# Moving two thirds of the modulation vector's matrix-vector products from the preceding feed-forward stage into the layer that uses them

## The chip, the cores and the metric

One core of a Trainium2 chip runs the whole program. The metric is the device time of one execution in microseconds (us); where several executions are given, their median counts. A core has five engines that run their own instruction streams in order and wait for each other by semaphores: TensorE (PE: matmuls; its weight loads are shown as PEld), VectorE (DVE), ScalarE (ACT), GpSimd (POOL) and SyncE (SP), which here issues all loads and stores.

## The reference, cut to what matters

The program is one inference step through two trunk layers for 640 tokens (512 latent, 128 context) of width 1024. In each layer a conditioning vector is turned into six modulation vectors of 1024 each (shift, scale and gate of the mixers, shift, scale and gate of the feed-forward part), for the latent and for the context condition:

```
def adaln(cond, w_ada, b_ada):
    m = jax.nn.silu(cond) @ w_ada + b_ada          # w_ada (1024, 6144), one per layer
    return [t[:, None, :] for t in jnp.split(m, 6, axis=-1)]

sh1, sc1, g1, sh2, sc2, g2 = mod
h = rms_norm(x) * (1 + sc1) + sh1                  # blocks 0-7 (shift) and 8-15 (scale)
... four mixers from h @ w_in: latent attention (MLA), a recurrence (HGRN), neighbourhood
    attention (NA), grouped-query attention (GQA)
x = x + g1 * merge_branches(...)                   # blocks 16-23
h2 = rms_norm(x) * (1 + sc2) + sh2                 # blocks 24-31 and 32-39
x = x + g2 * ((silu(gate_ffn) * a) @ w_ffn_out)    # blocks 40-47
```

A block is 128 entries of the modulation vector, so a layer has 48 blocks, and a block's weights are 512 KB.

## The kernel before, in words

Activations lie with channels on the 128 partitions and the 640 tokens along the free axis, in two halves of 384 and 256 columns. Every matmul of the large projections runs three times on values split in a high and a low part, so TensorE has by far the most work. A layer goes through these stages: a preparation of the latent attention (`mla_pre`), then sixteen mixers `j` = 0 to 15 in the order MLA 0-3 (phase `ph` 0), HGRN 4-7 (phase 1), NA 8-11 (phase 2), GQA 12-15 (phase 3), then the merge, the output projection `out`, the second norm, and the feed-forward stage.

A mixer is a Python generator that yields between its pieces: an attention mixer (`attn_pair`) 18 times, an HGRN mixer (`hgrn_mix`) 11 times. `weave` runs one such generator and, after each yield, as much of a filler (the projections for the next mixer, the gates, the branch projections) as keeps pace. In an attention mixer a unit is: scores on PE into `pss`; row maximum on DVE (`sm`, L218); exponential on ACT (`P`, L235); reciprocal and scaling on DVE (L231, L232); a unit later the transposes on PE (`pst`, L81) and their split into `ph` (ACT) and `pl` (DVE, L176). Each weight block is loaded by SP into `wraw` (two buffers, L117) and split by ACT and DVE into `whi` and `wlo` (L123). In an HGRN mixer seven levels follow each other, each with matmuls into `pss`, a masked copy on DVE (`hA`, L804) and small products on DVE and POOL (L817 to L824); its last DVE instruction is L882.

The modulation blocks are made by `ada_tail` as row products on DVE, not on PE. For each item it loads a piece of a block (`ada`, L982) and multiplies it on DVE with the two conditions and sums it (L984; two of these *products* per item, each followed by a short read of the accumulator, `aacc`). With `parts` = 4 an item is 128x256 (128 KB), with 2 it is 128x512 (256 KB). The conditions themselves are loaded from `crow` at the start of each part (L978). The weights go through a ring of `depth` pieces, so the load of an item waits until DVE is done with the item `depth` before it, and SP's later loads stand behind it.

The Python order is not the order of execution: when the program is built, a scheduler orders the instructions of every engine. It may put an instruction ahead of others that were written earlier, where its inputs are there and the engine would have nothing else. In the kernel before, `along` draws three items of layer 0's blocks 16 to 39 after each yield of mixers 4 to 7; the feed-forward stage of layer 0 makes layer 0's blocks 40 to 47 and all 48 blocks of layer 1, four items after each hidden block (`hidden`) and two after each output block (`back`). Layer 1 makes none in its own stages. That makes the two layers a natural pair for comparison: the same work with and without the products.

Of the kernel before, what the change touches and what calls it, by code (L numbers as in the profile page):

```python
# [7 lines left out]
F32 = mybir.dt.float32  # L8
# [19 lines left out]
NH = FFN // 128  # L28
# [36 lines left out]
class Trunk:  # L65
# [1025 lines left out]

    def along(self, main, side, n):

        try:
            while True:
                yield next(main)
                for _ in range(n):
                    next(side, None)
        except StopIteration as e:
            return e.value  # L1100
# [22 lines left out]
    def mixers(self, l, first):  # L1123
# [27 lines left out]

        self.weave(rest(), early(), 15360 * len(EARLY), 70000)
        outs, nxt = None, []
        for j in range(16):
# [9 lines left out]
            main = mix.pop(j)()  # L1164
            if l == 0 and 4 <= j < 8:
                if j == 4:
                    ada = self.ada_tail(0, 16, 40, 4, 2)
                main = self.along(main, ada, 3)
            nxt.append(self.weave(main, f, wp + wm, steps[ph]))
            if j % 4 == 3:  # L1170
                outs, nxt = self.split_outs(nxt), []
        for d in range(8):
            for _ in self.merge(l, order[3], d, outs, gates):
                pass
        self.drop(outs)

    def layer(self, l, hs, first):
# [49 lines left out]
        nxt = l + 1 < self.depth  # L1227
        def ada():
            if l == 0:
                yield from self.ada_tail(0, 40, 48, 2, 4, True)  # L1230
            if nxt:
                yield from self.ada_tail(l + 1, 0, 48, 2, 4, True)

        ada = ada()

        def back(halves, last=False):
            for m in range(8):
# [6 lines left out]
                for c0, c1 in halves:  # L1244
                    self.resid(x[m], self.gemm(w, [fs[j] for j in range(g0, g1)], c0, c1), l, 40, m, c0, c1)
                    yield 3 * (g1 - g0) * (c1 - c0)
                if g1 < NH:
                    for _ in range(2):
                        next(ada, None)

        ws = []
        for g0, g1 in KGROUPS:
            for j in range(max(g0, 2), g1):
                sum(hidden(j, HALVES, None))
                for _ in range(4):
                    next(ada, None)
            if g1 < NH:
                sum(back(HALVES))
                self.drop([fs[j] for j in range(g0, g1)])
# [39 lines left out]
    def run(self):  # L1299
        nc, tc, A = self.nc, self.tc, self.A  # L1300
        with (
# [24 lines left out]
            self.trash = cst.tile([128, 256], BF16, name="trash")  # L1326
            self.aacc = cst.tile([128, 192], F32, name="aacc")
            self.mod = [cst.tile([128, 48, 2], F32, name=f"mod{l}") for l in range(self.depth)]
# [205 lines left out]
```

## Time and profile before

| what | value |
|---|---|
| time before, median of 3 runs | 3157.28 us (3156.32 to 3160.29) |
| the profiled execution's own time | 3160.58 us |
| its span in the profile | 3158.8 us |
| mean granted TensorE clock | 0.994 of full |
| PE busy | 3042.6 us (96%) |
| DVE busy | 2183.3 us (69%) |
| ACT busy | 1467.5 us (46%) |
| POOL busy | 286.0 us (9%) |

The span is what the views below divide into stretches, counted from its first instruction; 1.8 us of the execution lie outside it. PE's ends are modelled, so a busy PE is not PE at its peak.

### The profile page before, as it was taken

How to read it: one execution, taken by the hardware profiler on the slowest of the kernel's cores; microseconds unless marked ns; L12 is line 12 of the kernel's file. 1: busy time of each engine (PE TensorE's matmuls, PEld its weight loads, DVE VectorE, ACT ScalarE, POOL GpSimd, SP SyncE). 2: the span in 40 equal slices, each digit the busy share in tenths (PEclk: the TensorE clock that was granted, in tenths of full speed). 3: DMA queues.
4: the chain of work that ended last, by engine and by line, in shares of the span. 5: the costliest groups of instructions: out<-in, count | busy, mean ns of one | idle time of the engine just before them, and what ended most of it. 6: DMA issues, size and time to landing. Idle time of an engine off the chain costs nothing.

```text
span 3158.8 us, 54167 instructions
## 1 busy us (share of the span) xinstructions
PE 3042.6 (96%) x20898; PEld 2934.2 (93%) x20898; DVE 2183.3 (69%) x4894; ACT 1467.5 (46%) x3090; POOL 286.0 (9%) x301
## 2 busy tenths in 40 slices
PE   8999989899999999999998999999999999999998
PEld 4899988899899999999998999989988999999998
DVE  5676988877877577676867776678778766533335
ACT  4565433556765352121346654446576644422222
POOL 1100222110111010000001002221011100000000
PEclk9999999999999999999999999999999999999999
DMA  6211333232111345454521112213311124322222
GB/s 216 66 62 63 118 114 113 81 103 89 48 41 59 124 154 161 147 163 146 167 91 60 60 61 74 73 58 97 98 61 44 46 68 160 101 81 70 78 76 72
DMA packets 135121, 297.16 MB, mean 94 GB/s; under 512 B 15888, under 2 KB 53584, under 8 KB 134864
## 3 DMA queue, kind: packets, MB, share of 16 engines
q1 hardware_dynamic: 134864, 293.71, 28.9%
q8 instruction: 165, 2.70, 0.4%
q14 instruction: 92, 0.75, 0.1%
HBM read 276.70 MB, written 16.95 MB: 93 GB/s over the span
## 4 chain that ended last, share of the span: by engine, by line
PE 71%; DVE 15%; ACT 5%; issue 4%; DMA 4%; POOL 1%; SPq 0%; DVEq 0%; ACTq 0%; POOLq 0%
PE psg L78 58%; PE pss L78 7%; PE pst L81 3%; PE pst L78 3%; DVE wlo L123 2%; DVE trash L984 2%; ACT P L235 1%; DVE pl L176 1%; DMA ada<-in_w_ada 1%; ACT whi L84 1%; DVE nx L1054 1%; DMA wada<-in_w_adak 1%; PE pst L167 1%; DVE sm L218 1%; DVE P L232 1%
## 5 line engine op out<-in xcount | busy, mean ns | idle before, releaser
L78 PE MATMUL psg<-hh,whi 128*128 128x384 f32 (+1 forms) x3776 | 1121.1, 315 | 7.5 <-DVE ft L1209 4.5
L78 PE MATMUL psg<-hl,whi 128*128 128x384 f32 (+1 forms) x3776 | 1109.0, 312 | 2.8 <-DVE hl L1056 2.4
L78 PEld LDWEIGHTS psg<-hh,whi 128*128 128x128 f32 x3776 | 717.0, 190 | 10.6 <-DVE ft L1209 5.1
L78 PEld LDWEIGHTS psg<-hl,whi 128*128 128x128 f32 x3776 | 717.3, 190 | 4.7 <-DVE hl L1056 3.1
L78 PE MATMUL psg<-hh,wlo 128*128 128x384 f32 (+1 forms) x3744 | 649.5, 312 | 0.0
L84 ACT ACTIVATE whi<-wraw 128x1024 fp32r<-128x1024 f32 (+3 forms) x402 | 380.7, 947 | 457.4 <-PE psg L78 365.7
L78 PEld LDWEIGHTS psg<-hh,wlo 128*128 128x128 f32 x3744 | 569.5, 190 | 0.0
L123 DVE TENSOR_TENSOR wlo<-wraw,whi 128x1024 fp32r<-128x1024 f32 (+3 forms) x398 | 455.1, 1144 | 123.0 <-ACT whi L84 112.4
L235 ACT ACTIVATE P<-pss,sm 128x768 f32<-128x768 f32 (+2 forms) x240 | 163.0, 680 | 202.2 <-DVE sm L218 114.5
L176 DVE TENSOR_TENSOR pl<-pst,ph 128x384 fp32r<-128x384 f32 (+2 forms) x408 | 196.4, 510 | 24.6 <-ACT ph L84 20.2
L84 ACT ACTIVATE ph<-pst 128x384 fp32r<-128x384 f32 (+2 forms) x408 | 170.4, 457 | 49.4 <-PE pst L81 46.2
L81 PE MATMUL pst<-ident,P 128*128 128x128 f32 x1104 | 168.3, 275 | 16.5 <-DVE of L242 11.3
L1070 DVE SCALAR_TENSOR_TENSOR xr<-psg,mod,xr 128x128 f32<-128x128 f32 (+1 forms) x192 | 78.6, 436 | 152.0 <-PE psg L78 151.9
L218 DVE TENSOR_REDUCE sm<-pss 128x1 f32<-128x768 f32 x128 | 122.0, 953 | 53.6 <-PE pss L78 52.6
L984 DVE CUSTOM_DVE_ANT_0 yada<-ada 128x512 f32<-128x512 f32 x224 | 154.4, 689 | 5.1
L81 PEld LDWEIGHTS pst<-ident,P 128*128 128x128 f32 x1104 | 125.6, 140 | 31.2 <-DVE of L242 17.6
L78 PE MATMUL psg<-oTh,whi 128*128 128x384 f32 (+1 forms) x512 | 153.0, 316 | 0.1
L78 PE MATMUL psg<-oTl,whi 128*128 128x384 f32 (+1 forms) x512 | 152.7, 314 | 0.0
L78 PE MATMUL psg<-fh,whi 128*128 128x256 f32 (+1 forms) x512 | 148.1, 308 | 0.0
L78 PE MATMUL psg<-fl,whi 128*128 128x256 f32 (+1 forms) x512 | 148.1, 308 | 0.0
L84 ACT ACTIVATE fh<-fy 128x384 fp32r<-128x384 f32 (+1 forms) x88 | 41.4, 471 | 179.4 <-DVE fy L1211 179.4
L1211 DVE SCALAR_TENSOR_TENSOR fy<-ft,psg 128x384 f32<-128x384 f32 (+1 forms) x88 | 42.8, 487 | 112.3 <-PE psg L78 111.7
(324 smaller groups left out, 5181.3 us busy)
## 6 DMA issues: line engine op xcount, KB each, us to landing
wraw<-in_w_f SPq DMA_DIRECT2D x128, 512.0 KB, 3.4
wraw<-in_w_in SPq DMA_DIRECT2D x88, 512.0 KB, 3.4
wraw<-in_w_gate SPq DMA_DIRECT2D x64, 512.0 KB, 3.3
ada<-in_w_ada SPq DMA_DIRECT2D x112, 256.0 KB, 3.1
wraw<-in_w_br SPq DMA_DIRECT2D x64, 256.0 KB, 2.6
wraw<-in_w_out SPq DMA_DIRECT2D x32, 512.0 KB, 3.3
ada<-in_w_ada SPq DMA_DIRECT2D x96, 128.0 KB, 2.3
gd<-gt SPq DMA_DIRECT2D x28, 320.0 KB, 2.2
```

What stands on the lines that cost most here:

```text
L78: self.nc.tensor.matmul(out, lhsT, rhs, start=start, stop=stop)
L81: self.nc.tensor.transpose(out, in_, self.ident)
L84: self.nc.scalar.activation(out, in_, AF.Copy, scale=scale)
L123: nc.vector.tensor_sub(lo[:, :n], raw[:, :n], self.r(hi[:, :n]))
L167: self.nc.tensor.transpose(ps[:, i * rows : (i + 1) * rows], t[:rows, c0 + i * 128 : c0 + (i + 1) * 128], self.ident[:rows, :rows])
L176: self.nc.vector.tensor_sub(lo, src, self.r(hi))
L218: nc.vector.tensor_reduce(nm, S[:, 0:n], axis=AX.X, op=ALU.max, negate=True)
L232: nc.vector.tensor_scalar_mul(P[:, p0 : p0 + n], P[:, p0 : p0 + n], l)
L235: self.nc.scalar.activation(P, S, AF.Exp, bias=nm, accum_out=l)
L984: nc.vector.tensor_tensor_reduce(out=y, in0=w, in1=c, scale=1.0, scalar=0.0, op0=ALU.mult, op1=ALU.add, accum_out=acc[:, b, k, j : j + 1])
L1070: self.nc.vector.scalar_tensor_tensor(x[:, a:b], ps[:, a - c0 : b - c0], mod[:, b_g + m, j : j + 1], x[:, a:b], op0=ALU.mult, op1=ALU.add)
L1211: nc.vector.scalar_tensor_tensor(y[:, 0:n], tg[:, 0:n], 0.5, pa, op0=ALU.mult, op1=ALU.mult)
```

## The change

`along` takes a fraction instead of a whole number: it now draws `a` items in `b` yields (3 in 5), with a count that goes on from mixer to mixer. Both layers make blocks 16 to 47 as 128 items of 128x256, drawn along the mixers of phases 0, 2 and 3, that is MLA, NA and GQA; what is left after mixer 15 is made before the merge. The feed-forward stage of layer 0 keeps only blocks 0 to 15 of layer 1 (32 items of 128x512, two after each hidden block and none after `back`). The accumulator tile `aacc` grows from 192 to 256 columns. In all the program has 96 items of 128x256 and 112 of 128x512 before, and 256 and 32 now; the bytes loaded for them are the same (42 MB).

```diff
@@ -1089,12 +1089,13 @@
             sum(fill)
         return res
 
-    def along(self, main, side, n):
+    def along(self, main, side, count, a, b):
 
         try:
             while True:
                 yield next(main)
-                for _ in range(n):
+                count[0] += 1
+                for _ in range(count[0] * a // b - (count[0] - 1) * a // b):
                     next(side, None)
         except StopIteration as e:
             return e.value
@@ -1150,6 +1151,7 @@
             mix[0] = yield from first
 
         self.weave(rest(), early(), 15360 * len(EARLY), 70000)
+        ada, count = self.ada_tail(l, 16, 48, 4, 2), [0]
         outs, nxt = None, []
         for j in range(16):
             ph, q = divmod(j, 4)
@@ -1162,13 +1164,13 @@
             p = prep(j + 1) if j < 15 else None
             f = self.blend(p, wp * (3 if j == 11 else 1), merges(j, outs), wm)
             main = mix.pop(j)()
-            if l == 0 and 4 <= j < 8:
-                if j == 4:
-                    ada = self.ada_tail(0, 16, 40, 4, 2)
-                main = self.along(main, ada, 3)
+            if ph != 1:
+                main = self.along(main, ada, count, 3, 5)
             nxt.append(self.weave(main, f, wp + wm, steps[ph]))
             if j % 4 == 3:
                 outs, nxt = self.split_outs(nxt), []
+        for _ in ada:
+            pass
         for d in range(8):
             for _ in self.merge(l, order[3], d, outs, gates):
                 pass
@@ -1225,13 +1227,7 @@
         self.weave(self.norm_mod(hs, x, l, 24, 32, *HALVES[1]), some(HALVES[0]), 96 * n0, 6)
         sum(some(HALVES[1]))
         nxt = l + 1 < self.depth
-        def ada():
-            if l == 0:
-                yield from self.ada_tail(0, 40, 48, 2, 4, True)
-            if nxt:
-                yield from self.ada_tail(l + 1, 0, 48, 2, 4, True)
-
-        ada = ada()
+        ada = self.ada_tail(l + 1, 0, 16, 2, 4, True) if nxt else iter(())
 
         def back(halves, last=False):
             for m in range(8):
@@ -1244,15 +1240,12 @@
                 for c0, c1 in halves:
                     self.resid(x[m], self.gemm(w, [fs[j] for j in range(g0, g1)], c0, c1), l, 40, m, c0, c1)
                     yield 3 * (g1 - g0) * (c1 - c0)
-                if g1 < NH:
-                    for _ in range(2):
-                        next(ada, None)
 
         ws = []
         for g0, g1 in KGROUPS:
             for j in range(max(g0, 2), g1):
                 sum(hidden(j, HALVES, None))
-                for _ in range(4):
+                for _ in range(2):
                     next(ada, None)
             if g1 < NH:
                 sum(back(HALVES))
@@ -1324,7 +1317,7 @@
                 return t
 
             self.trash = cst.tile([128, 256], BF16, name="trash")
-            self.aacc = cst.tile([128, 192], F32, name="aacc")
+            self.aacc = cst.tile([128, 256], F32, name="aacc")
             self.mod = [cst.tile([128, 48, 2], F32, name=f"mod{l}") for l in range(self.depth)]
             self.crow = dr.tile([2, D], F32, name="crow")
             c = const("cond", "cond")
```

What the scheduler makes of it is seen in the built order. On DVE, in the first MLA mixer of layer 1, around the first two row maxima (`sm<-pss`), before:

```order
L267 RECIPROCAL sm<-sm 128x2
L268 TENSOR_TENSOR P<-P,sm 128x256
L176 TENSOR_TENSOR mv<-psg,mv 128x64
L218 TENSOR_REDUCE sm<-pss 128x1
L176 TENSOR_TENSOR mv<-psg,mv 128x64
L231 RECIPROCAL sm<-sm 128x1
L232 TENSOR_SCALAR P<-P,sm 128x768
L176 TENSOR_TENSOR pl<-pst,ph 128x256
```

and now, at the same place (the `ISA` rows of L984 are the products and the reads of their accumulator):

```order
L218 TENSOR_REDUCE sm<-pss 128x1
L984 ISA trash,aacc<-ada 128x256
L984 ISA aacc 128x1
L176 TENSOR_TENSOR pl<-pst,ph 128x256
L984 ISA trash,aacc<-ada 128x256
L984 ISA aacc 128x1
L231 RECIPROCAL sm<-sm 128x1
L232 TENSOR_SCALAR P<-P,sm 128x768
```

Products moved in between the row maximum and the reciprocal, and to other places of the unit. On DVE, in the first HGRN mixer of layer 1, from its second to its third level, before:

```order
L817 TENSOR_TENSOR hq<-hq,hT 128x40x2x4
L819 TENSOR_TENSOR hq<-hq,hT 128x40x8
L824 TENSOR_TENSOR hT<-hT_22024 128x40 x2
L123 TENSOR_TENSOR wlo<-wraw,whi 128x512
L804 COPY_PREDICATED hA<-hmask,pss 128x640
```

and now:

```order
L824 TENSOR_TENSOR hT<-hT_21922 128x40 x2
L984 ISA trash,aacc<-ada 128x256
L984 ISA aacc 128x1
L984 ISA trash,aacc<-ada 128x256
L984 ISA aacc 128x1
L984 ISA trash,aacc<-ada 128x256
L984 ISA aacc 128x1
L123 TENSOR_TENSOR wlo<-wraw,whi 128x512
L984 ISA trash,aacc<-ada 128x256
L984 ISA aacc 128x1
L804 COPY_PREDICATED hA<-hmask,pss 128x640
```

So products now stand in layer 1's HGRN mixers, although none is drawn along them: the scheduler took them forward. On SP, in layer 1 at the start of the MLA mixers (weight loads of L117, stores of gates of L895), before:

```order
L117 DMA wraw<-in_w_k 128x128
L895 DMA gd_98<-gt 128x640
L117 DMA wraw<-in_w_v 128x256
L117 DMA wraw<-in_w_gate 128x1024
L117 DMA wraw<-in_w_qn 128x256
```

and now:

```order
L117 DMA wraw<-in_w_k 128x128
L978 DMA ada<-crow 128x256 x2
L982 DMA ada<-in_w_ada 128x256
L895 DMA gd_98<-gt 128x640
L117 DMA wraw<-in_w_v 128x256
L982 DMA ada<-in_w_ada 128x256 x2
L117 DMA wraw<-in_w_gate 128x1024
L982 DMA ada<-in_w_ada 128x256 x2
L117 DMA wraw<-in_w_qn 128x256
```

The loads of the items moved in ahead of weight loads of the same stage. Counted over DVE's whole order, with the stretches named by the DVE rows at which they begin (each MLA mixer at its L264, and the HGRN mixers by their ends at L882), the products of 128x256 stand thus:

| stretch of a layer | before, layer 0 | before, layer 1 | now, layer 0 | now, layer 1 |
|---|---|---|---|---|
| preparation, up to the first MLA mixer | 0 | 0 | 11 | 10 |
| MLA mixers 1 to 3 | 0 | 0 | 82 | 83 |
| A: MLA mixer 4 and HGRN mixer 1 | 68 | 0 | 100 | 100 |
| B: HGRN mixer 2 | 62 | 0 | 54 | 54 |
| C: HGRN mixer 3 | 51 | 0 | 9 | 9 |
| D: HGRN mixer 4 | 11 | 0 | 0 | 0 |
| NA and GQA mixers | 0 | 0 | 0 | 0 |

Of the 82 and 83 in MLA mixers 1 to 3, 47 and 45 stand between a row maximum and its reciprocal. The products of 128x512 in the feed-forward stage of layer 0 are 224 before and 64 now.

## Rows read from the trace of the kernel before

**Rows 1.** The page: busy time, share of the span and instructions of each engine.
```profile
PE 3042.6 (96%) x20898; PEld 2934.2 (93%) x20898; DVE 2183.3 (69%) x4894; ACT 1467.5 (46%) x3090; POOL 286.0 (9%) x301
```

**Rows 2.** Busy time by stretch: layer 0's, then layer 1's.
```profile
core 0: us, PE busy (x) PEld busy (x) DVE busy (x) ACT busy (x) POOL busy (x), PEclk, DMA share, GB/s
...
278.90:608.90 330.00, 302.01 (x2103) 289.67 (x2101) 279.08 (x766) 136.00 (x269) 68.52 (x68) 0.98 0.32 102
...
1045.70:1612.40 566.70, 563.57 (x3836) 562.10 (x3835) 411.08 (x888) 178.97 (x267) 12.85 (x12) 1.00 0.47 151
1698.20:1845.90 147.70, 144.62 (x1007) 138.15 (x1008) 114.33 (x244) 93.60 (x224) 0.00 (x0) 0.99 0.19 64
1845.90:2145.90 300.00, 294.92 (x2103) 284.64 (x2102) 197.97 (x378) 136.65 (x269) 67.01 (x68) 1.00 0.21 66
2145.90:2582.40 436.50, 421.35 (x2954) 403.36 (x2953) 333.35 (x808) 266.92 (x650) 46.41 (x51) 1.00 0.21 67
2582.40:3147.90 565.50, 563.32 (x3835) 561.89 (x3833) 259.26 (x437) 173.10 (x260) 8.18 (x8) 1.00 0.28 91
```

**Rows 3.** The same view: stretches A to D of layer 0, then of layer 1.
```profile
278.90:419.20 140.30, 133.29 (x927) 128.97 (x925) 113.14 (x288) 60.37 (x120) 24.41 (x22) 0.99 0.31 97
419.20:495.80 76.60, 69.18 (x484) 67.69 (x485) 65.88 (x199) 26.79 (x48) 16.57 (x17) 0.96 0.38 118
495.80:560.90 65.10, 57.02 (x395) 54.04 (x394) 58.24 (x174) 24.49 (x45) 17.30 (x17) 0.97 0.35 111
560.90:608.90 48.00, 42.52 (x302) 38.97 (x300) 41.82 (x110) 24.35 (x56) 10.23 (x12) 1.00 0.24 75
1845.90:1977.90 132.00, 131.38 (x931) 128.09 (x931) 85.93 (x156) 60.42 (x120) 23.42 (x22) 1.00 0.21 66
1977.90:2044.30 66.40, 66.32 (x478) 64.59 (x477) 39.18 (x75) 27.05 (x48) 16.03 (x17) 1.00 0.22 73
2044.30:2099.20 54.90, 52.91 (x385) 50.99 (x384) 36.50 (x69) 25.20 (x48) 17.23 (x17) 1.00 0.18 57
2099.20:2145.90 46.70, 44.31 (x315) 40.97 (x313) 36.36 (x83) 23.98 (x53) 10.32 (x12) 1.00 0.22 67
```

**Rows 4.** The products of 128x256: duration in ns (min/median/max), first and last start.
```profile
L984 DVE CUSTOM_DVE_ANT_0 trash<-ada x192: 402/424/1772, 324.8 to 572.8; 128x256 bf16<-128x256 f32 x192
```

**Rows 5.** What PE waited for, layer 0 from 278.9 to 608.9 us: total, times, longest.
```profile
PE pss L78 <- DVE hSf L852: 10.5, 3, 5.4
PE pss L78 <- DVE hA L804: 3.8, 6, 0.9
PE pss L81 <- DVE hon L871: 3.6, 3, 1.9
```

**Rows 6.** What DVE waited for, the same stretch.
```profile
DVE trash L984 <- DMA ada<-in_w_ada: 9.0, 13, 1.8
DVE trash L984 <- DMA ada<-crow: 6.7, 5, 1.7
```

**Rows 7.** What SP's loads waited for, the same stretch.
```profile
SPq L982 <- DVE aacc L984: 88.7, 63, 4.8
SPq L117 <- DVE wlo L123: 52.3, 15, 17.1
SPq L117 <- DVE aacc L984: 23.0, 11, 4.0
```

**Rows 8.** What DVE waited for, MLA mixers 1 to 3 of layer 1 (1698.2 to 1845.9 us).
```profile
DVE sm L231 <- ACT P L235: 15.1, 16, 1.1
DVE sm L218 <- PE pss L78: 6.7, 9, 1.1
...
DVE sm L267 <- ACT P L235: 1.7, 2, 0.9
```

**Rows 9.** What PE waited for, the same stretch of layer 1.
```profile
PE pst L81 <- DVE of L242: 2.3, 4, 0.6
```

**Rows 10.** Busy time in the end of layer 1's preparation (columns as in group 2).
```profile
1620.00:1698.20 78.20, 70.64 (x479) 67.07 (x479) 51.98 (x117) 48.12 (x115) 14.94 (x16) 0.98 0.24 79
```

## The prediction

> **What bounds the kernel now.** I read the page first: TensorE is busy 96% of the span, VectorE 69% [rows 1]. So nearly all the time is PE's, and a change that moves only DVE work and loads can act in one way alone: by making PE wait more, or less, for DVE. Where that happens is not seen in the mean, so I cut the span into stages and laid layer 0 beside layer 1, which do the same work [rows 2]. The reader should see two things there. The feed-forward stage is 566.7 us in layer 0 and 565.5 in layer 1, with PE busy 563.6 and 563.3: layer 0 carries 224 products that layer 1 hasn't (DVE 411.1 against 259.3 us), and they cost 1.2 us in all. And the stretch from the fourth MLA mixer to the first NA mixer is 330.0 us in layer 0 and 300.0 in layer 1: here 192 products cost 30.0 us. DVE is busy 279.1 against 198.0 us there, so a product with its accumulator read is 81.1 / 192 = 0.422 us of DVE, which agrees with its own median duration of 424 ns [rows 4].
>
> The waits then say how it becomes time: in that stretch of layer 0 PE waits for DVE's results in the HGRN chain (hSf 10.5, hA 3.8, hon 3.6 us) [rows 5]. DVE itself waits 9.0 + 6.7 = 15.7 us for the products' loads [rows 6]. SP stands 88.7 us in front of product loads, and weight loads behind them wait 23.0 us on products [rows 7]; in front of its other weight loads it waits for buffers.
>
> **A scale for the cost.** The stretch splits into four at the ends of the HGRN mixers, and each layer 0 piece has its layer 1 twin without products [rows 3]. For each I set the products' DVE time against the time that DVE is idle in the twin, and read off what the piece lost:
>
> A: 140.3 - 132.0 = 8.3 us for 68 products, 28.7 us of DVE for 132.0 - 85.9 = 46.1 idle (62% filled): 0.122 us lost for each product.
> B: 76.6 - 66.4 = 10.2 for 62; 26.2 for 27.2 idle (96%): 0.165.
> C: 65.1 - 54.9 = 10.2 for 51; 21.5 for 18.4 idle (117%): 0.200.
> D: 48.0 - 46.7 = 1.3 for 11; 4.6 for 10.3 idle (45%): 0.118.
>
> The loss rises with the filling, and isn't small even at half. These rates hold everything that comes with a product: DVE's delay, the ring's waits, SP's blocked weight loads, and the granted clock, which in B and C of layer 0 is 0.96 and 0.97 of 2.4 GHz, a mean with short spells at 1.2 GHz after PE stood, and 1.00 in their twins. So I don't price those apart.
>
> **The change, part by part.** What decides is where the built order puts the products, by the counts of the table above, not where they are drawn. NA and GQA get none in either layer, so their 436.5 us [rows 2] stay. Each layer now has 82 or 83 in MLA mixers 1 to 3, 100 in A, 54 in B, 9 in C, none in D, and 10 or 11 in the preparation.
>
> *Taken away*: layer 0's stretch loses its present 192 products: -30.0 us. The feed-forward stage loses 160 of 224: 1.2 x 160/224 = -0.9 us. The work that hides the rest is PE itself, which never runs short there. Were that cover gone, all the DVE time of the 64 left would show, 64 x (411.1 - 259.3)/224 = 43 us; PE's 99% says it isn't.
>
> *Added, MLA mixers 1 to 3* (147.7 us, DVE busy 114.3, idle 33.4 [rows 2]). 83 products are 35.0 us, more than the idle time. No row shows products in these mixers, so I bound it. From below: all idle time is used and only the excess shows, 1.6 us. From above: DVE is never busier than in layer 0's stretch, 279.1/330.0 = 84.6%, so the mixers last (114.3 + 35.0)/0.846 = 176.5, +28.8 us. Between them: 46 products stand between a row maximum and its reciprocal, where DVE now idles 15.1 + 1.7 = 16.8 us for the exponential [rows 8]; they need 19.4, so 2.6 us of theirs is left over. The other 37 I charge at the rate of B and C for a filling of 105%, 0.18 us: 6.7. Together 9.3 us. I take this value: the order fits more than half into waits that exist, and PE waits on DVE for little there today (2.3 us on the largest [rows 9]); but 84.6% filled DVE is nearer to what the next mixers show than 100%, so not less.
>
> *Added, A, B, C*: A at 100 x 0.422/46.1 = 92% filled: between the rates of 62 and 96%, 0.160, so 16.0 us. B at 54: 84%, 0.150, 8.1 us. C at 9: 21%, no rate that low, 0.11 at most from D, 1.0 us. Sum 25.1 (at the mean rate 30.0/192 it would be 163 x 0.156 = 25.5).
>
> *Added, preparation*: DVE is idle 78.2 - 52.0 = 26.2 us in its last part [rows 10]; 11 products at 0.11, 1.2 us. Nothing, if they fall in PE's shadow; 4.6 if each shows in full.
>
> *SP's queue*: 160 more loads of 128 KB and 80 fewer of 256 KB. DMA engines are at most 0.47 busy in any of these stretches [rows 2], so the bytes cost nothing. What stands behind a product load now is the next MLA mixer's weights and the gates' stores; its cost is in the rates. That two ring slots stay taken through MLA, the wider `aacc`, and blocks 16 to 47 of layer 1 being made only in layer 1 (their first reader is the output projection, two phases after the last product) I cost at nothing: no row shows a wait on them.
>
> A layer's cost is 9.3 + 25.1 + 1.2 = 35.6 us. Two layers: 71.2; less 30.0 and 0.9: **+40.3 us**. Layer 0 ends about 5 us later than now, layer 1 about 35. The profiled execution's 3160.6 us becomes 3200.9; it stands 3.3 us above the median of the runs, so against the median I forecast 3157.3 + 40 = **3197 us**, its own range 3186 to 3212 as the 9.3 and the 25.1 are each off by up to a third. Chance 0.50.
>
> **The rivals.**
>
> *Neighbours, not filling (0.19).* GpSimd is busy 68.5 us in the stretch where products cost 30.0, and 0.00 us in MLA mixers 1 to 3 [rows 2]; single products take up to 1772 ns against a median of 424 [rows 4]. If the loss comes from products that run beside GpSimd, those in MLA mixers 1 to 3 and the preparation are free and only 163 in a layer pay 0.156: 25.5 us, two layers 51, less 30.9: +20, **3177 us**. Against it: A has the same share of GpSimd (24.4 of 140.3, or 17%) as B (22%) and yet loses a quarter less for each product; the rates follow the filling. The Trainium skill, "SBUF — State Buffer", section "Who interferes with whom", says that a VectorE instruction with two SBUF inputs and a GpSimd instruction that reads SBUF block each other for the whole instruction; a product has two such inputs. The long tail of durations agrees with that rule, and by it this rival's time would be the right one.
>
> *Saturation (0.15).* MLA mixers 1 to 3 reach the upper bound, +28.8, since weight loads come late behind product loads as well: a layer 28.8 + 25.1 + 1.2 = 55.1, +79 in the end, **3236 us**; half of the way from the forecast, 3217. For it: DVE is overfilled by 1.6 us even if no wait of its own is left, and a DVE that runs behind lets SP fall behind.
>
> *The other side: it was the loads (0.08).* Half of the 30.0 us is DVE standing for the ring, 15.7 us [rows 6]. If the new order gives the loads time to land, the rest is 14.3/192 = 0.074 a product; 163 of them cost 12.1 us, those in MLA's waits none: 24.3 - 30.9 = -6.6, **3151 us**, faster. It decides where a layer's whole cost falls below (30.9 - 6.3)/2 = 12.3 us. Against it: SP's order now has product loads ahead of nearly every weight load of these mixers, and the ring is as short as before.
>
> *It does what the words say*: the attention stages take the products and HGRN is free of them. If hidden, that would be -30.9, 3126 us. The built order excludes it: 163 of 256 products stand in stretches A to C.
>
> *No change that can be told (0.08).* Costs between the last two cases and the forecast that happen to meet the gain, 15 us a layer.
>
> **How the numbers follow.** 0.2%, 6.3 us, is about what these runs can tell from no change. Faster by more needs the loads' case: 0.08. Within it: 0.08. The forecast, the neighbours and saturation are all slower: 0.84. For 8 in 10 I leave out the faster case, part of the one without change, and the last third of saturation: 3160 to 3228 us.
>
> **What the profile after would show.** MLA mixers 1 to 3 of both layers near 157 us, with the wait of the reciprocal for the exponential gone from DVE's list; at 148 or 149 the neighbours' or the loads' case is right, at 170 saturation. The stretch A to D near 325 us in both layers, layer 0's slightly below its 330.0, layer 1's up from 300.0, with PE waits on hSf and hA in A and B of layer 1 and none in C and D. NA with GQA unchanged at 436.5 us. The feed-forward stage of layer 0 within 1 us of layer 1's. DVE's wait for `ada` loads of the order of 10 to 25 us a layer. The forecast is wrong if the MLA mixers behave like the feed-forward stage, where 224 products vanish beside a PE that has enough to do, or if the shifted order of PE's own instructions gains or loses by itself.

## The result and the profile after

The changed kernel takes 3177.97 us (median of 4 runs, 3175.21 to 3182.16) where the kernel before took 3158.02 beside it: ratio 1.006, 95% interval 1.0045 to 1.0075. It is slower by about 20 us; 39 to 40 had been forecast. The profiled execution took 3175.21 us with a span of 3173.3, 14.5 more than before's span; it lies 2.8 below its median and before's 2.6 above, which makes up the 20.

The page's line of busy times, which answers to [rows 1]:

```profile
PE 3048.2 (96%) x20898; PEld 2937.9 (93%) x20898; DVE 2191.8 (69%) x5216; ACT 1464.6 (46%) x3086; POOL 294.4 (9%) x301
```

Nothing is to be seen in it: shares stay the same to the percent. The stretches, cut as in [rows 2, 3] (layer 0's MLA mixers 1 to 3, A to D, feed-forward stage, then layer 1's MLA mixers 1 to 3, A, B, C, D, A to D, NA with GQA):

```profile
core 0: us, PE busy (x) PEld busy (x) DVE busy (x) ACT busy (x) POOL busy (x), PEclk, DMA share, GB/s
133.80:285.80 152.00, 145.37 (x1009) 137.16 (x1009) 141.87 (x410) 93.30 (x225) 0.00 (x0) 1.00 0.31 99
...
285.80:604.60 318.80, 297.99 (x2101) 287.23 (x2100) 262.86 (x710) 136.97 (x270) 70.17 (x68) 0.99 0.31 98
...
1041.20:1606.20 565.00, 562.69 (x3830) 561.31 (x3829) 305.86 (x564) 178.22 (x266) 12.79 (x12) 1.00 0.35 112
...
1693.90:1846.00 152.10, 145.08 (x1008) 136.66 (x1008) 142.59 (x412) 93.10 (x225) 0.00 (x0) 1.00 0.31 100
1846.00:1990.50 144.50, 134.57 (x924) 131.00 (x923) 124.80 (x357) 60.74 (x121) 24.57 (x22) 0.96 0.34 110
1990.50:2060.30 69.80, 66.42 (x477) 64.61 (x477) 60.51 (x180) 27.14 (x48) 16.57 (x17) 1.00 0.35 111
2060.30:2113.90 53.60, 52.59 (x380) 50.60 (x381) 41.75 (x92) 24.11 (x44) 18.46 (x17) 1.00 0.23 74
2113.90:2163.10 49.20, 45.27 (x321) 42.30 (x321) 36.89 (x85) 25.11 (x57) 10.27 (x12) 1.00 0.26 74
1846.00:2163.10 317.10, 298.85 (x2101) 288.53 (x2101) 263.94 (x710) 137.10 (x270) 69.86 (x68) 0.98 0.31 98
2163.10:2597.50 434.40, 421.52 (x2960) 403.22 (x2959) 333.55 (x808) 266.28 (x649) 48.98 (x51) 1.00 0.21 67
```

Read down the lengths. MLA mixers 1 to 3 went from 147.7 to 152.0 and 152.1. A to D went from 330.0 to 318.8 in layer 0 and from 300.0 to 317.1 in layer 1. NA with GQA is 2.1 us shorter in layer 1, the feed-forward stage 1.7 and 0.7. DVE in MLA is busy 142.6 of 152.1 us, 94%, and PE still loses only 4.4. A product with its read takes (142.59 - 114.33) / 83 = 0.341 us of DVE there, not 0.422, so the 83 fill 85% of the 33.4 idle and not 105%.

A was the largest term, so I cut it once more, 46 us after its start, where the products of before begin in layer 0 (324.8 us [rows 4]). First the two parts in the kernel before, layer 1, without products:

```profile
1845.90:1891.80 45.90, 45.36 (x309) 44.14 (x309) 29.25 (x53) 22.83 (x48) 4.69 (x3) 1.00 0.15 48
1891.80:1977.90 86.10, 86.02 (x624) 83.95 (x624) 56.68 (x103) 37.59 (x73) 18.73 (x19) 1.00 0.24 76
```

and now:

```profile
1846.00:1892.00 46.00, 44.33 (x302) 43.21 (x302) 40.74 (x118) 22.81 (x50) 6.60 (x5) 1.00 0.28 89
1892.00:1990.50 98.50, 90.24 (x623) 87.80 (x621) 84.06 (x240) 37.93 (x72) 17.97 (x18) 0.95 0.37 119
```

This is a cut by time, so the first part is 46 us long in both. The same instruction of PE, the first on `wlo` behind the scores, starts 45.8 us after the start of A before and 46.6 now: a third of the products cost 0.8 us there, though DVE is 89% busy, and 11.7 of the 12.5 us come later.

Cut at the same work, at the first matmul of HGRN mixer 1 (`pss<-hQ,hkk`) and at GpSimd's second instruction on `hkk` behind the levels, A has three parts. Before, layer 1:

```profile
1845.90:1909.20 63.30, 62.76 (x441) 61.12 (x441) 42.37 (x76) 32.87 (x70) 7.11 (x5) 1.00 0.17 53
1909.20:1952.59 43.39, 43.31 (x310) 42.71 (x309) 28.43 (x54) 16.03 (x31) 12.45 (x14) 1.00 0.25 81
1952.59:1977.90 25.31, 25.31 (x184) 24.26 (x183) 15.12 (x27) 11.52 (x20) 3.86 (x4) 1.00 0.26 75
```

and now:

```profile
1846.00:1916.22 70.22, 65.17 (x440) 63.37 (x439) 60.27 (x175) 33.10 (x71) 7.30 (x5) 0.95 0.31 101
1916.22:1959.58 43.36, 43.28 (x310) 42.72 (x309) 41.23 (x112) 16.02 (x31) 13.22 (x15) 1.00 0.37 119
1959.58:1990.50 30.92, 26.12 (x179) 24.92 (x177) 23.30 (x72) 11.62 (x20) 4.05 (x4) 0.94 0.38 116
```

The middle part, the seven levels, lost nothing, with 29 products in it, DVE busy 95% of the time and GpSimd 30%. The 12.5 us are the 6.9 up to the first level and the 5.6 behind the last one; layer 0 has 7.8, 0.2 and 5.2.

The 6.9 hang on one row maximum of MLA mixer 4. Before, DVE took it as soon as its scores were there, the first row; now it first makes two products among other work, waits 1.60 us for the conditions' row and makes two more products:

```profile
1891.94 0.96 DVE L218 TENSOR_REDUCE sm<-pss 128x1 f32<-128x768 f32 x1 [0.64 <-PE pss L78]
...
1896.73 0.43 DVE L984 CUSTOM_DVE_ANT_0 trash<-ada 128x256 bf16<-128x256 f32 x1 [1.60 <-DMA ada<-crow]
...
1897.55 0.95 DVE L218 TENSOR_REDUCE sm<-pss 128x1 f32<-128x768 f32 x1
```

ACT waits 4.4 us for it and makes `hvf`, a tile of HGRN mixer 1, behind it; PE waits 3.4 us for `hvf`. No instruction of GpSimd runs between 1892.7 and 1919.8 us, and none of the 49 products up to the first level took more than 0.43 us. Layer 0 has the same stand (3.5 us) behind the same wait (1.59).

What a product beside GpSimd looks like, and what then stands behind it, is in the timeline. GpSimd where the third part begins (start, length, engine, line, operation):

```profile
1959.58 1.76 POOL L765 TENSOR_TENSOR hkk<-hk 128x640 f32<-128x640 f32 x1
```

and DVE in 9 us around it:

```profile
1958.65 1.24 DVE L984 CUSTOM_DVE_ANT_0 trash<-ada 128x256 bf16<-128x256 f32 x1
...
1959.94 1.69 DVE L984 CUSTOM_DVE_ANT_0 trash<-ada 128x256 bf16<-128x256 f32 x1
...
1964.43 0.42 DVE L984 CUSTOM_DVE_ANT_0 trash<-ada 128x256 bf16<-128x256 f32 x1 [1.86 <-DMA ada<-in_w_ada]
...
1966.39 1.22 DVE L123 TENSOR_TENSOR wlo<-wraw,whi 128x1024 fp32r<-128x1024 f32 x1
1967.53 0.34 DVE L852 SCALAR_TENSOR_TENSOR hSf<-hSf,hT,pss 128x128 f32<-128x128 f32 x1
```

The product of 1.69 us instead of 0.42 ends 0.3 us after GpSimd's instruction; the two long ones together take 2.1 us more than two others. Behind them DVE works off six more products, waits 1.86 us for a load among them, and comes late to `hSf`, the state of the recurrence, for which PE waits 2.7 us. PE's waits in A to D of layer 1, which answer to [rows 5]:

```profile
PE pss L78 <- DVE hSf L852: 5.1, 2, 2.7
PE pst L167 <- ACT hvf L84: 3.4, 1, 3.4
PE pss L78 <- DVE hA L804: 3.1, 4, 1.4
```

A stand costs more than itself. In the 11 us after the wait of 3.4 us (the first row), and in 13 us around the one for `hSf` above (the second), the granted clock is

```profile
1901.00:1912.00 11.00, 10.85 (x57) 10.57 (x58) 8.10 (x26) 4.38 (x11) 0.00 (x0) 0.72 0.48 165
1967.00:1980.00 13.00, 12.08 (x76) 11.58 (x77) 9.25 (x32) 2.39 (x8) 0.02 (x1) 0.87 0.41 126
```

that is, part of each at 1.2 GHz instead of 2.4. From the matmul that waited for `hvf` to the next ones on `ph` and `mv`, the same work, PE takes 6.65 us where it took 3.94. Over all of A the granted clock of 0.96 would be 5.8 us of work at full speed (0.04 of 144.5); PE's busy time rose by 3.2, from 131.4 to 134.6.

### The profile page after: what moved, and what is told of

It reads as the page before. It is cut to its first block, busy times and chain, and to the rows that moved or that the text cites. A ratio compares the mean times of both kernels' runs of the same rounds, so it can differ in the third digit from the quotient of the medians.

```text
span 3173.3 us, 54661 instructions
## 1 busy us (share of the span) xinstructions
PE 3048.2 (96%) x20898; PEld 2937.9 (93%) x20898; DVE 2191.8 (69%) x5216; ACT 1464.6 (46%) x3086; POOL 294.4 (9%) x301
## 4 chain that ended last, share of the span: by engine, by line
PE 68%; DVE 18%; ACT 5%; DMA 4%; issue 3%; POOL 0%; SPq 0%; DVEq 0%; ACTq 0%; POOLq 0%
PE psg L78 57%; PE pss L78 6%; DMA ada<-in_w_ada 2%; PE pst L78 2%; PE pst L81 2%; DVE wlo L123 2%; DVE trash L984 2%; DVE pl L176 2%; ACT P L235 2%; DVE P L232 1%; DVE sm L218 1%; ACT whi L84 1%; DVE nx L1054 1%; PE pst L167 1%; ACT ph L84 1%
## 5 line engine op out<-in xcount | busy, mean ns | idle before, releaser
L984 DVE CUSTOM_DVE_ANT_0 trash<-ada 128x256 bf16<-128x256 f32 x512 | 234.0, 457 | 51.6 <-DMA ada<-in_w_ada 38.3
L176 DVE TENSOR_TENSOR pl<-pst,ph 128x384 fp32r<-128x384 f32 (+2 forms) x408 | 197.0, 510 | 17.6 <-ACT ph L84 14.5
```

Source lines behind the costliest of these rows:

```text
L176: self.nc.vector.tensor_sub(lo, src, self.r(hi))
L984: nc.vector.tensor_tensor_reduce(out=y, in0=w, in1=c, scale=1.0, scalar=0.0, op0=ALU.mult, op1=ALU.add, accum_out=acc[:, b, k, j : j + 1])
```

## The experiments

Throughout, my theory is that of the forecast: a product costs what DVE's filling makes it cost. The rivals were the loads, GpSimd, and later the place where a product stands. Times are medians beside runs of the kernel before; the ratio is to these. The median of the kernel before was 3158.0 to 3160.6 us beside the different runs, so two times that weren't taken side by side can differ by 2 to 3 us without a cause in the kernel.

**What is there to lose: no products, loads alone, products alone, a deeper ring.** Four kernels, each the change with one edit. Blocks 16 to 47 without loads and products (their values are left out):

```diff
-                for j, c in enumerate((c0, c1)):
+                for j, c in enumerate((c0, c1) if last else ()):
```

with `if last:` ahead of the load as well.

> All loads and products of the items along the mixers are left out (blocks 16 to 47 of the modulation are then only the bias): the floor. By the twins in the kernel before, a layer without products has 300.0 us in A to D and 147.7 in MLA mixers 1 to 3: 3158 - 30 = 3128, and the change's products cost the rest, 50 us, or 25 a layer. All theories agree; it sets the scale for the next three.

Measured 3125.8 us, ratio 0.9887 (0.9873 to 0.9902). This is the floor for everything below. The loads alone (the values again left out):

> The loads of the items stay, with their ring, but no product reads them (blocks 16 to 47 are then only the bias). Filling and neighbours: the loads cost nothing by themselves, the floor within 5 us, 3128 to 3133. Loads (SP's queue held up): 10 us or more above the floor; but without products the ring is freed by the loads themselves, so this shows only what the DMA traffic costs, not the waits for DVE.

Measured 3133.9 us, 0.9912 (0.9898 to 0.9927): 8 us over the floor, between the two expectations. Products alone, with the condition's row in place of the loaded piece (so other values):

> The products stay, but read the rows of the conditions that lie in SBUF, and no pieces of weights are loaded (the modulation is then wrong in blocks 16 to 47). Since nothing waits for a ring, the order takes more of them forward: 94 in MLA mixers 1 to 3, 137 in A, 11 in B, none in C. Loads: DVE's 14 to 18 us of waiting for loads in A to D are gone in each layer: about 3178 - 30 = 3148. Filling: A is 137 x 0.40/46 = 119% filled and costs 0.2 a product, 27 us, so 35 us a layer: 3195 or more.

Measured 3172.38 us, 1.0034 (1.0021 to 1.0047): 47 us over the floor; neither theory had expected it. A took 149.2 us in layer 1: 0.13 for each of its 137 products, not 0.2. Four pieces in the ring instead of two (`ada_tail(l, 16, 48, 4, 4)`):

> The ring has four pieces instead of two; nothing is left out. The order takes more products forward: 93 in MLA mixers 1 to 3, 140 in A, 12 in B. Loads: a load has twice the time to land and SP stands less before it, so A to D lose most of their 14 to 18 us of waits: 3150 to 3155. Filling: as without loads, 3190 or more, since A is 119% filled.

Measured 3175.75 us, 1.0046 (1.0031 to 1.0061), not to be told from the change, and again neither theory had expected it. DVE's waits for loads in layer 1's A to D are 0.6 us in all instead of 15.7, and nothing is gained; A took 146.3 us, 0.10 for each of 140 products. In this kernel 41 of them stand in the levels, with DVE 97% busy, and PE stands 3.0 of their 49.8 us: what was free for 29 isn't for 41. So most of the price is the products', not their loads' (8 of 52 us by themselves), nor the short ring's, and the forecast's scale doesn't hold where DVE is fullest. The floor's stretches in layer 1 (MLA 1 to 3, A, B, C, D, A to D, NA with GQA) are the scale for what follows:

```profile
1667.30:1813.80 146.50, 143.51 (x1007) 136.77 (x1007) 115.26 (x247) 92.87 (x225) 0.00 (x0) 1.00 0.20 64
1813.80:1945.70 131.90, 131.28 (x931) 128.03 (x930) 86.20 (x155) 60.71 (x121) 23.43 (x22) 1.00 0.22 67
1945.70:2012.00 66.30, 66.22 (x478) 64.57 (x477) 39.54 (x73) 26.95 (x48) 16.09 (x17) 1.00 0.21 70
2012.00:2064.30 52.30, 51.94 (x378) 50.00 (x377) 35.30 (x68) 23.92 (x44) 16.79 (x17) 1.00 0.19 58
2064.30:2113.60 49.30, 45.25 (x322) 42.31 (x320) 36.76 (x84) 24.90 (x57) 10.32 (x12) 1.00 0.25 74
1813.80:2113.60 299.80, 294.68 (x2103) 284.91 (x2101) 197.79 (x376) 136.47 (x270) 66.64 (x68) 1.00 0.22 67
2113.60:2549.30 435.70, 421.62 (x2961) 403.37 (x2960) 334.73 (x810) 266.02 (x649) 47.90 (x51) 1.00 0.21 66
```

C and D differ from [rows 3] by -2.6 and +2.6 with no product anywhere, so their new lengths in the changed kernel don't come from products. NA with GQA is 0.8 us shorter here than in [rows 2], so part of its 2.1 us doesn't either.

**One layer alone.** The change for layer 0 only; layer 1's 48 blocks in the feed-forward stage as before.

```diff
-        ada, count = self.ada_tail(l, 16, 48, 4, 2), [0]
+        ada, count = self.ada_tail(l, 16, 48, 4, 2) if l == 0 else iter(()), [0]
```

> Layer 0 makes its blocks 16 to 47 along its attention mixers as in the change, but all 48 blocks of layer 1 are made in layer 0's feed-forward stage again, as before. The built order puts layer 0's products where the change has them (82 in MLA mixers 1 to 3, 100, 54 and 9 in A, B and C) and none in layer 1. If the pieces add up, the change's layer 1 pieces (MLA +4.4, A to D +17.1, preparation +1.9, NA and GQA -2.9 us) go away and the feed-forward stage takes back at most 1: about 3178 - 20 = 3158, or up to 5 us under the kernel before, since layer 0's own pieces gave -5 in the change's trace. All theories of why a product costs what it does agree here; above 3165 the pieces don't add.

Measured 3157.1 us, 0.9987 (0.9978 to 0.9996). The layers' parts add: what the change loses against the kernel before is lost in layer 1.

**GpSimd or DVE's time.** A row sum of the loaded piece in place of the product (other values), one SBUF input instead of two:

```diff
+                    else:
+                        nc.vector.tensor_reduce(acc[:, b, k, j : j + 1], w, axis=AX.X, op=ALU.add)
```

> Each product of 128x256 is replaced by a plain row sum of the loaded piece (its result is then not the modulation): one SBUF input instead of two, the loads as they are. The order stays nearly as in the change (87 to 89 in MLA mixers 1 to 3, 102 in A, 56 to 58 in B, none in C). Neighbours (the cost comes from products beside GpSimd): stretches A to D fall from 317 to 319 us to nearly the 300 us without products, so about 3178 - 30 = 3148. Filling (the cost follows DVE's load): the same as the change within 6 us, 3172 to 3184, if a row sum lasts as long as a product. Loads (the cost is DVE standing for the ring): the same, 3178.

Measured 3153.62 us, 0.9982 (0.9972 to 0.9991): 24 us of the loss are gone. But a row sum has no read of an accumulator behind it, and DVE was busy 116.7 us in A instead of 124.8, so this run doesn't separate the two. The next one levels DVE's time: two row sums for each product, over 256 and over 72 columns.

```diff
+                        nc.vector.tensor_reduce(self.pad, w[:, 0:72], axis=AX.X, op=ALU.add)
```

> Each product of blocks 16 to 47 and the read of its accumulator are replaced by two row sums of the loaded piece, over 256 and over 72 columns, so that VectorE has about the same time per piece (0.47 us back to back) but never two SBUF inputs in one instruction; the loads stay. What is left out: these blocks' values are not the modulation. The built order is 10 in the preparation, 66 in MLA mixers 1 to 3, 91 in A, 48 in B, 33 in C, 8 in D. Theory 1 (VectorE's time is what costs, wherever it falls on a chain that TensorE waits for): A 142 to 146 us, B 68 to 71, C 54 to 57, the time 3170 to 3182 us, like the change. Theory 2 (two-input instructions and GpSimd block each other): no row sum much above its own length beside GpSimd, A at most 140 and B at most 67 as with the single row sum, the time 3148 to 3158. In MLA mixers 1 to 3, where GpSimd does nothing, both expect 151 to 153 us.

Measured 3160.56 us, 1.0004 (0.9995 to 1.0013), between the two ranges and nearer to the second theory's. Its A and B in layer 1:

```profile
1839.20:1977.60 138.40, 132.21 (x932) 128.29 (x930) 125.56 (x338) 60.77 (x121) 24.09 (x22) 1.00 0.33 107
1977.60:2045.20 67.60, 65.76 (x474) 64.44 (x475) 59.65 (x170) 27.05 (x48) 16.74 (x17) 1.00 0.33 110
```

DVE and GpSimd are as busy as in the change's A, but A is 6.1 us shorter, B 2.2, and the clock is 1.00. MLA mixers 1 to 3, where both theories expected 151 to 153, took 153.1 us in layer 0 and 148.9 in layer 1, so this run differs from the change by some us where GpSimd stands still, too. The instructions on the pieces in A and B, duration min/median/max, in this kernel:

```profile
L990 DVE TENSOR_REDUCE pad<-ada x139: 200/218/229, 1839.1 to 2042.2; 128x1 f32<-128x72 f32 x139
L989 DVE TENSOR_REDUCE aacc<-ada x139: 397/409/421, 1839.6 to 2042.3; 128x1 f32<-128x256 f32 x139
```

and in the change:

```profile
L984 DVE CUSTOM_DVE_ANT_0 trash<-ada x155: 396/424/1699, 1845.7 to 2059.1; 128x256 bf16<-128x256 f32 x155
```

Nothing above 421 ns against 1699. The rule of the Trainium skill ("SBUF — State Buffer", section "Who interferes with whom": a VectorE instruction with two SBUF inputs and a GpSimd instruction that reads SBUF block each other) agrees with these rows, and so does the timeline above. But the three parts of this A, cut at the same work, don't put the gain there:

```profile
1839.20:1904.70 65.50, 63.06 (x441) 60.92 (x440) 59.29 (x159) 32.81 (x71) 7.15 (x5) 1.00 0.30 98
1904.70:1949.48 44.78, 43.33 (x310) 42.68 (x309) 41.84 (x112) 16.10 (x31) 13.05 (x15) 1.00 0.35 113
1949.48:1977.60 28.12, 25.81 (x186) 24.68 (x184) 24.43 (x69) 11.86 (x20) 3.89 (x4) 1.00 0.37 120
```

Of the 6.1 us, 4.7 are gained up to the first level (5.6 of 6.2 in layer 0), where the change had no product lengthened; the levels are 1.4 longer; behind them 2.8 are gained. A row sum doesn't read the conditions, so this kernel has no wait for `crow` ahead of the row maximum, and it writes one column where a product writes 256. With these differences and the order's (91 pieces in A instead of 100) the run doesn't separate GpSimd from DVE's time. The block with GpSimd can be worth at most the 2.8 in A, and by the two long products of the timeline about 2.

**The same products elsewhere: a ring taken anew.** The ring's tiles are taken from the pool again for each quarter, which holds the products back in the built order: 67 in MLA mixers 1 to 3, 61 in A, none in B to D, 58 in NA, 70 in GQA. In both layers:

> The ring is taken anew for each quarter of the items, from the slot freed last, so a quarter can't run ahead of its place in the program. The order now has 67 products in MLA mixers 1 to 3, 61 in A, none in B to D, 58 in NA and 70 in GQA. Filling: MLA +3.5, A 61 at 56% filled, 0.11, +7, NA and GQA 128 at about 43%, 0.06, +8: 18 to 19 us a layer against the change's 24: 3166. Neighbours: GpSimd stands still in MLA mixers and most of NA and GQA, so only A's products beside HGRN pay, 3 to 8 us a layer: 3140 to 3150. Loads: if a gated ring gives more time, near 3155.

Measured 3174.05 us, 1.004 (1.0025 to 1.0055), above all three expectations. B to D are at the floor, but MLA took 152.7 us, A 135.3, NA with GQA 449.4 in layer 1. In layer 0 alone:

> As the gated ring, but for layer 0 alone, with all of layer 1's blocks in layer 0's feed-forward stage. Filling: the kernel before less its 30 us, plus 18: 3146. Neighbours: less 30, plus 3 to 8: 3131 to 3136. In both it is faster than before and than the change; it would be the version to keep.

Measured 3154.26 us, 0.9981 (0.9971 to 0.9991), again above both. NA and GQA charged about 0.11 us a product (13.7 us for 128 over the floor) with DVE's own work at 77% there, and MLA mixers 1 to 3 0.09 (6.2 for 67). By itself the 0.11 would fit the forecast's scale: 128 products fill about half of the idle time, and D had 0.118 at 45%. But the next run charges half of that for more products in the same stages.

**The same products elsewhere: another output tile.** The change with one word more: outputs of the products, which nobody reads, go to the common pool (as f32 rows) and not to `trash`.

```diff
-        ada, count = self.ada_tail(l, 16, 48, 4, 2), [0]
+        ada, count = self.ada_tail(l, 16, 48, 4, 2, True), [0]
```

> The change with one difference: the products of blocks 16 to 47 write their output rows, which nobody reads, into tiles of the common pool and not into one fixed tile, as the feed-forward stage's products do. The draw and the pieces are the same, but the built order now keeps the products where they are drawn: in each layer 4 in the preparation, 58 in MLA mixers 1 to 3, 24 in A, none in B, C and D, 86 in the NA and 66 in the GQA mixers, the last 18 or 22 behind them. Theory 1 (a product costs about 0.12 us in NA and GQA, as in the kernel whose ring was taken anew): MLA 3, A 1 to 3, NA and GQA 18, so 22 to 24 us a layer and 3166 to 3176 us, like the change. Theory 2 (beside a busy GpSimd a product is dear, in NA and GQA it costs what 44 and 10 wide ones cost in the run before, about 0.05 us each): 3 + 1 + 7 = 11 us a layer, 3145 to 3152 us.

Measured 3154.63 us, 0.9986 (0.9977 to 0.9995): 23 us less than the change, nearer to the second range than to the first. MLA 1 to 3, A, A to D and NA with GQA of layer 1:

```profile
1684.80:1833.30 148.50, 143.40 (x1000) 135.73 (x1000) 134.22 (x362) 92.35 (x224) 0.00 (x0) 1.00 0.26 89
1833.30:1966.40 133.10, 132.27 (x937) 129.03 (x938) 94.10 (x204) 60.85 (x122) 22.74 (x22) 1.00 0.25 81
1833.30:2134.10 300.80, 295.65 (x2110) 285.92 (x2110) 205.90 (x426) 136.91 (x271) 65.96 (x68) 1.00 0.22 74
...
2134.10:2578.40 444.30, 424.39 (x2960) 403.44 (x2959) 386.97 (x1154) 264.25 (x649) 51.11 (x51) 1.00 0.28 91
```

With no product in the HGRN mixers, A to D is back within 1.0 us of the floor, where the change had lost 17.3. The 170 products from there to the merge cost 444.3 - 435.7 = 8.6 us, 0.05 each, and the 82 in the four MLA mixers 2.0 + 1.0, 0.04 each. A product itself is as long as in the change (median 418 ns in MLA mixers 1 to 3, where the change's mean is 420), so it is the order that gains. This is the change as its words describe it, and it is no slower than before.

**Wide pieces, and fewer blocks.** Pieces of 128x512 in both layers (`ada_tail(l, 16, 48, 2, 2, True)`, 3 draws in 10):

> The change with pieces of 128x512 for blocks 16 to 47 (128 products of twice the length a layer, drawn 3 in 10, output rows in the common pool). Built order of a layer: 2 in the preparation, 30 in MLA mixers 1 to 3, 10 in A, none in B to D, 44 in NA, 34 in GQA, the last 8 behind them. If the price is that of the run with layer 0's 96 wide products (about 9 us of layer 0 for 96): 12 us a layer, 3146 to 3152 us, and the same as the run with pooled narrow ones within 4 us if only the place matters. If the number of instructions matters, this one is 5 to 12 us below that one.

Measured 3139.15 us, 0.9937 (0.9921 to 0.9954): 15 us less than the run before, more than I had expected of fewer instructions. Between the profiles 12.4 of 15.4 us are saved ahead of layer 1's first MLA mixer and 3.0 behind it; no single wait accounts for it. Then blocks 16 to 39 of layer 0 alone, the rest in the feed-forward stage as before, first with the change's narrow pieces and `trash`:

```diff
+        ada, count = self.ada_tail(l, 16, 40, 4, 2) if l == 0 else iter(()), [0]
...
+            if l == 0:
+                yield from self.ada_tail(0, 40, 48, 2, 4, True)
+            if nxt:
+                yield from self.ada_tail(l + 1, 0, 48, 2, 4, True)
```

> Only layer 0's blocks 16 to 39 are made along its mixers (192 products instead of 256, the same draw of 3 in 5); its blocks 40 to 47 and all of layer 1's go back to the feed-forward stage, as before. The built order of layer 0 is 11 in the preparation, 82 in MLA mixers 1 to 3, 97 in A and 2 in B. Theory 1 (what a product costs depends on the stage and on how full VectorE is there): preparation +2, MLA +4.4, A +12 to 13 over the times without products, B, C and D at nothing, so layer 0 costs 18 to 20 us instead of 30, and the time is 3145 to 3151 us. The mean rate of my forecast (0.156 us a product in A to D, 9.3 in MLA): 1.2 + 9.3 + 15.5 = 26, the time 3153 us.

Measured 3146.54 us, 0.9961 (0.9948 to 0.9973), in the first theory's range: MLA 1 to 3 took 151.8, A 142.4 for 97 products, 10.5 over the floor. With pooled outputs:

> As the run with 96 wide products in layer 0 alone (3134.9 us), but with 192 narrow ones of 128x256, output rows in the common pool: 4 in the preparation, 60 in MLA mixers 1 to 3, 22 in A, none in B to D, 86 in NA, 20 in GQA. If only the place matters, 3133 to 3138 us; if the number of instructions or VectorE's time does (96 more reads and starts of 0.05 to 0.08 us each, 5 to 8 us more of VectorE), 3138 to 3144.

Measured 3139.2 us, 0.9939 (0.9924 to 0.9954), in the second range, 1 us above the first. The 7 us against the kernel ahead come with the output tile and the order that goes with it. And with wide pieces:

> As the run before, but the 192 products of 128x256 are 96 of 128x512, drawn 3 in 10, with their output rows in the common pool, as the feed-forward stage's have them. The built order of layer 0 is 2 in the preparation, 30 in MLA mixers 1 to 3, 10 in A, none in B to D, 44 in the NA and 10 in the GQA mixers. Theory 1 by place: MLA 30 x 0.1 = 3 us, A 1 to 2, NA and GQA 54 x 0.24 = 13 if a wide product there costs twice a narrow one (0.12), so 17 to 18 us in all and the time 3143 to 3149. If a product's cost is the number of its instructions and not its length, NA and GQA take 6 to 7 and the time is 3137 to 3143. If a wide product costs more than two narrow ones since it holds VectorE longer at a time (0.7 us), above 3151.

Measured 3134.91 us, 0.9927 (0.9914 to 0.9941), the fastest that computes everything, 9 us over the floor by the medians and 13 by the ratios; below all three ranges that I had expected. A to D and NA with GQA of its layer 0:

```profile
280.00:579.10 299.10, 294.52 (x2102) 284.79 (x2100) 201.29 (x393) 137.31 (x270) 68.03 (x68) 1.00 0.22 70
...
579.10:1021.70 442.60, 424.58 (x2959) 404.88 (x2959) 362.36 (x923) 263.18 (x649) 47.33 (x51) 1.00 0.26 83
```

A to D is at the floor; most of what is left to pay is in NA with GQA, 6.9 us over the floor's 435.7 for 54 wide products (4.9 over the 437.7 of this kernel's own layer 1). Wide against narrow is 4 us here, with intervals that overlap.

## Why the prediction was right and wrong

Right: slower, inside the wide range (3160 to 3228); the built order and not the words of the change set the place; layer 0 gained and layer 1 lost; the wait of the reciprocal for the exponential (16.8 us in [rows 8]) disappeared from DVE's list in MLA 1 to 3, and the products left in the feed-forward stage stay hidden. Wrong: the size, outside the forecast's own 3186 to 3212 us, and the mechanism that gave it.

| term, a layer | forecast | measured, layers 0 and 1 |
|---|---|---|
| preparation | +1.2 | +2.6, +1.9 |
| MLA mixers 1 to 3 | +9.3 | +4.3, +4.4 |
| A, against [rows 3] layer 1 | +16.0 | +13.1, +12.5 |
| B | +8.1 | +4.6, +3.4 |
| C and D | +1.0 | +1.1, +1.2 |
| NA with GQA | 0 | -0.9, -2.1 |
| feed-forward | -0.9 and 0 | -1.7, -0.7 |

With the 30.0 us that layer 0 had lost before, the measured terms give 23.1 + 20.6 - 30.0 = +13.7 us of the 14.5 between the spans, where the forecast's gave +40.3.

The step that failed is **A scale for the cost**: the loss for each product, read off four pieces of layer 0 and set against DVE's filling. It gave 0.16 us for A at 92% and 0.15 for B at 84%, and 0.18 for the 37 products of MLA that found no wait. Measured were 0.125 to 0.131 in A, hardly more than the 0.122 at 62%; 0.06 to 0.085 in B; and 0.05 for all of MLA, though DVE is fuller there than in A. The levels of HGRN mixer 1 took 29 products for nothing with DVE 95% busy. What a product costs is not read off DVE's filling: PE lost time where one late result of DVE stood between it and its next work, at a row maximum ahead of `hvf` and at `hSf`. Three things were mixed in the rates:

1. *The cut of A was too coarse.* Before, all 68 products of layer 0's A stood behind its first 46 us: 28.7 us of them for 86.1 - 56.7 = 29.4 idle, 98% filled and not 62%, for 8.3 us. Now 33 stand in the first part for 0.8 us, and 67 in the second for 11.7, 0.175 each: as full as before, and dearer by two fifths.
2. *GpSimd.* I gave this rival 0.19 and argued that A and B have the same share of GpSimd but not the same loss. The long products are real, but most stand where nothing is lost; the two ahead of `hSf` make about 2 of the 12.5 us in A by their lengths, and B has such a pair too (1.24 and 1.70 us). Its forecast of 3177 us is what was measured, yet not by its own sum: it had MLA and the preparation free (they cost 6 to 7 us a layer) and A to C at 25.5 (A to D cost 17 to 19). Two errors that cancel: luck.
3. *The place.* With the same instructions, the run with pooled outputs pays 0.04 us in the MLA mixers and 0.05 in NA and GQA, where the change paid 0.14 for the 49 products between the start of MLA mixer 4 and the first level of HGRN mixer 1 and 0.25 for the 22 behind the last one. I carried the rates of layer 0's HGRN stretch to other mixers for want of rows. The kind of mixer doesn't set the price either: the ring taken anew paid 0.09 in MLA and 0.11 in NA and GQA.

The loads' case as forecast, 3151 us, is refuted by the three runs on loads and ring. Not cleared is the wait for the conditions' row: it stands ahead of the late row maximum in both layers, it is gone in the run with row sums, and no run took it away alone; in the run with pooled outputs such a wait of 2.4 us stands in an A that lost only 1.2. Saturation did not come: DVE at 94% in MLA lost 4.4 us. Its upper bound took the mean of layer 0's stretch, 84.6%, for the fullest that DVE gets, where [rows 3] has 89% in C (58.24 of 65.10). What stays open: how much of A's first 6.9 us is the products' time and how much the wait for the conditions; why the same stages charge half in the run with pooled outputs of what they charge with the ring taken anew; and what in the order makes wide pieces 15 us better in both layers.

## What to carry to other kernels

Price work that is added to a second engine by what it stands ahead of, not by how full the engine is: in HGRN mixer 1, 95% busy cost nothing in the levels, and ahead of one row maximum and of `hSf` 86% and 75% cost 6.9 and 5.6 us. Cut a stretch at the same work, not at the same time, and at every change of the work in it, before reading a rate from it, and make a floor kernel without the work first. Look at what pins filler work in the built order: here the output tile alone left 24 of 163 products a layer in A to C, and none in an HGRN mixer, worth 23 us.

## What the runs showed of the hardware

A 128x256 product of two SBUF operands beside a GpSimd instruction took up to 1.70 us instead of 0.42. The products in MLA mixers 1 to 3 of layer 1 in the changed kernel, where GpSimd does nothing (busy us, mean ns | idle before, and what ended it):

```profile
L984 DVE CUSTOM_DVE_ANT_0 trash<-ada 128x256 bf16<-128x256 f32 x83 | 34.9, 420 | 4.0 <-DMA ada<-in_w_ada 1.7 <-DMA ada<-crow 1.3
```

and those in A to D of the same layer, 483 ns in the mean:

```profile
L984 DVE CUSTOM_DVE_ANT_0 trash<-ada 128x256 bf16<-128x256 f32 x164 | 79.2, 483 | 19.0 <-DMA ada<-in_w_ada 14.1 <-DMA ada<-crow 1.6
```

After PE had stood for 3.4 us, the granted clock of the next 11 us was 0.72, and the matmuls from `hvf` to the next on `ph` took 6.65 us instead of 3.94.
